# Large GpSimd operations of an S5 mixer moved to VectorE, its small ones issued later, one gate strip moved behind the GLU

## The chip, the cores and the metric

One core of one Trainium2 chip. The metric is the device time of one execution of the program, in microseconds (us), lower is better. The core's engines are TensorE (PE in the rows, its weight loads PEld), VectorE (DVE), ScalarE (ACT), GpSimd (POOL) and SyncE (SP, which issues nearly all DMAs). Each runs its own instructions in a fixed order; semaphores tie them together.

## What is computed

A decoder layer on 1024 tokens of width 1024, all in fp32:

```
u_a, u_b, gate_a, gate_b = split(rms_norm(x) @ w_in + b_in)   # 4, 8, 8 and 8 strips of 128 columns
y  = s5(u_a)                  # complex diagonal recurrence, 32 groups, 64 states each
z  = gelu(y);  ya = z * sigmoid(z @ w_glu + b_glu)
xc = conv4(u_b);  r, i = sigmoid(xc @ w_r), sigmoid(xc @ w_i)   # per head
a  = exp(-8 r softplus(-lambda));  h_t = a h_(t-1) + sqrt(1 - a^2) i xc
m  = sigmoid(gate_a) * (ya @ w_a_out) + sigmoid(gate_b) * (h @ w_b_out)
x1 = x + m @ w_o;  x2 = x1 + swiglu(rms_norm(x1));  then a gated per-layer embedding and a last norm
```

The S5 parameters are made on the chip: `dt`, `mag = exp(lam_re*dt)`, sine and cosine of `lam_im*dt`, the powers of the complex step (`ar9`, `ai9`), and `fr, fi`, which need a division by `den = lam_re^2 + lam_im^2`.

## The kernel before, in words

**Layout.** Everything is held feature-major, as tiles of 128 partitions x 1024 tokens. A product of fp32 matrices is made of three products of split values (high and low part: `whi`, `wlo`, `xgh`, `xgl`). A strip of 128 output columns takes 8 blocks of 128 input rows, in two chunks of four; a chunk is loaded by SP, its high part made by ACT (L187), its low part by DVE (L188).

**Units.** TensorE's work is a list of units that `emit` (L320) writes out in order. u0 to u7 are the per-layer embedding's product; u8 to u11 the four `u_a` strips; then come `GATES_FIRST` = 10 gate strips (u12 to u21), four GLU units, one gate strip, eight `w_a_out` units, and eight `u_b` strips, each but the first followed by the small `r, i` product of the strip before it (`ri_mm` L586) and some by a gate strip (`UB_GATES`, after the strips 1, 3 and 5); then a gate strip, the last `r, i` product, and the last gate strip. After that come `w_b_out`, `w_o`, the feed-forward and the embedding's gate. Every unit's result is taken out of PSUM (its evacuation) only after the next unit's first chunk has been written out; PSUM has 4 buffers for units.

**Chains.** After each chunk `emit` calls `tick` (L244), and `tick` moves each running generator on by one `yield`. So the work beside the strips is written out in steps, one for each chunk: the norm's chain (`rstd_chain` L367), the S5 mixer (`s5_all` L1119 with `s5_params`, `s5_setup`, `s5_data`) and the recurrence (`lru` L605).

**Order on an engine.** A planner orders the instructions of each engine; what is written out first goes first among what is ready. All tiles of 128 x 1024 come from one pool of 43 buffers, and a buffer is given out in the order in which the tiles are written out. So an operation that needs a new tile can't go ahead of the tiles written out before it, such as the evacuation of the strip before. `high_priority` moves an instruction up, `issue_after(i)` holds one back until `i` was issued. The first 10 units have ACT and DVE in written order.

**The norm.** x is squared and summed on ACT and DVE (L410, L412), TensorE sums over partitions (L377), DVE scales it (L384), POOL takes the power -0.5 (L385), DVE spreads the result to a diagonal (L386), TensorE broadcasts it (L392), ACT copies it out as `rb`. TensorE has L392 between u8 and u9.

**S5.** `s5_params` works on 128 x 16 tiles, on POOL: two exponentials (L1062 to L1081), x and th (L1157), sine and cosine (L1163 to L1189), quadrants (L1192 on), powers (L1217 on), `den` and its reciprocal on DVE (L1241 to L1244), `fr`, `fi`, and the split angle `gh`, `gl` (L1259 to L1270): seven steps. Then a loop waits until the norm's result is known (`while "x" not in self.rstd`). Then: `bb` (L1279), `bd`, and `s5_setup` for each of two halves in five steps: the products `qr`; `qi` (DVE) and `wr, wi` (POOL, L1327 to L1332); transposes (L1343); small products (L1358); `ks`, with the DMAs of `km`. Then `s5_data` in seven steps for each half: loads and tables (L1384 to L1392 DVE, `m8` L1394, L1395 POOL), sine and cosine (ACT), `psv` (PE), four products (DVE L1437 to L1440) and sums (POOL L1442, L1443), two scans (L1445, L1446), four products (L1447 to L1450) and sums (POOL L1451, L1452), `psy` (PE L1465, L1470), and the store of Y. The second half runs one step behind the first. The units of the GLU are preceded by `pre_glu` (L666), which writes out all steps that S5 still has, then loads y, makes z = gelu(y) and splits it.

**Recurrence.** `lru` takes two strips at a time: a, a tanh (ACT), a squared (POOL L616), L619 (DVE), L621 and L626 (POOL), and the scan L630 (DVE).

Of the kernel before, what the change touches and what calls it, by code (L numbers as in the profile page):

```python
# [17 lines left out]
P = 128  # L18
# [15 lines left out]
GATES_FIRST = 10  # L34
UB_GATES = (1, 3, 5)
# [59 lines left out]
class Build:  # L95
# [271 lines left out]
    def rstd_chain(self, acc, put, n=L, lag=0, lag2=0):  # L367
# [67 lines left out]
    def plan(self):  # L435
# [169 lines left out]
        def lru(m0):  # L605
# [19 lines left out]
            for m in ms:  # L625
                nc.gpsimd.tensor_tensor(out=ri[m, 1], in0=ri[m, 1], in1=th.pop(m), op=ALU.mult)  # L626
# [25 lines left out]
        def load_z():  # L652
            for m in range(4):
# [4 lines left out]
                self.zs[m] = self.split(z, "z")  # L658
                yield
# [71 lines left out]
        def ev_b(m):  # L731
            def ev(ps):
# [6 lines left out]
                nc.gpsimd.tensor_tensor(out=g, in0=g, in1=gl.pop(("p", m)), op=ALU.add)  # L739
# [379 lines left out]
    def s5_all(self):  # L1119
        self.zs = {}  # L1120
# [23 lines left out]
    def s5_params(self):  # L1144
# [45 lines left out]

        n, b, hh = T("n"), T("b"), T("hh")
        e.tensor_scalar(out=n, in0=k, scalar1=0.25, scalar2=-0.375, op0=ALU.mult, op1=ALU.add)  # L1192
        e.tensor_scalar(out=n, in0=n, scalar1=MAGIC, scalar2=None, op0=ALU.add)
        e.tensor_scalar(out=n, in0=n, scalar1=-MAGIC, scalar2=-4.0, op0=ALU.add, op1=ALU.mult)
        e.tensor_tensor(out=n, in0=k, in1=n, op=ALU.add)
        e.tensor_scalar(out=hh, in0=n, scalar1=2.0, scalar2=None, op0=ALU.is_ge)
        e.tensor_scalar(out=b, in0=hh, scalar1=-2.0, scalar2=None, op0=ALU.mult)
        e.tensor_tensor(out=b, in0=n, in1=b, op=ALU.add)
        nb, ss, cs, sn, cn, w2 = T("nb"), T("ss"), T("cs"), T("sn"), T("cn"), T("w2")
        e.tensor_scalar(out=nb, in0=b, scalar1=-1.0, scalar2=1.0, op0=ALU.mult, op1=ALU.add)  # L1200
        e.tensor_scalar(out=ss, in0=hh, scalar1=-2.0, scalar2=1.0, op0=ALU.mult, op1=ALU.add)
        e.tensor_scalar(out=cs, in0=b, scalar1=-2.0, scalar2=1.0, op0=ALU.mult, op1=ALU.add)
        e.tensor_tensor(out=cs, in0=cs, in1=ss, op=ALU.mult)
        e.tensor_tensor(out=sn, in0=s, in1=nb, op=ALU.mult)
        e.tensor_tensor(out=w2, in0=c, in1=b, op=ALU.mult)
        e.tensor_tensor(out=sn, in0=sn, in1=w2, op=ALU.add)
        e.tensor_tensor(out=sn, in0=sn, in1=ss, op=ALU.mult)
        e.tensor_tensor(out=cn, in0=c, in1=nb, op=ALU.mult)
        e.tensor_tensor(out=w2, in0=s, in1=b, op=ALU.mult)
        e.tensor_tensor(out=cn, in0=cn, in1=w2, op=ALU.add)  # L1210
        e.tensor_tensor(out=cn, in0=cn, in1=cs, op=ALU.mult)
        yield

        ar9 = self.ar9 = self.small([P, 16, 9], name="ar9")
        ai9 = self.ai9 = self.small([P, 16, 9], name="ai9")
        pw = self.small([P, 16, 4], name="pw")
        e.memset(ar9[:, :, 0:1], 1.0)  # L1217
        e.memset(ai9[:, :, 0:1], 0.0)
        ar, ai = ar9[:, :, 1], ai9[:, :, 1]
        e.tensor_tensor(out=ar, in0=mag, in1=cn, op=ALU.mult)  # L1220
        e.tensor_tensor(out=ai, in0=mag, in1=sn, op=ALU.mult)
        for m in (1, 2, 4):

            lo, hi = slice(1, m + 1), slice(m + 1, 2 * m + 1)
            br = ar9[:, :, m:m + 1].to_broadcast([P, 16, m])
            bi = ai9[:, :, m:m + 1].to_broadcast([P, 16, m])
            e.tensor_tensor(out=ar9[:, :, hi], in0=ar9[:, :, lo], in1=br, op=ALU.mult)
            e.tensor_tensor(out=pw[:, :, :m], in0=ai9[:, :, lo], in1=bi, op=ALU.mult)
            e.tensor_tensor(out=ar9[:, :, hi], in0=ar9[:, :, hi], in1=pw[:, :, :m], op=ALU.subtract)
            e.tensor_tensor(out=ai9[:, :, hi], in0=ar9[:, :, lo], in1=bi, op=ALU.mult)  # L1230
            e.tensor_tensor(out=pw[:, :, :m], in0=ai9[:, :, lo], in1=br, op=ALU.mult)
            e.tensor_tensor(out=ai9[:, :, hi], in0=ai9[:, :, hi], in1=pw[:, :, :m], op=ALU.add)
        self.mag8 = T("mag8")
        e.tensor_tensor(out=self.mag8, in0=mag, in1=mag, op=ALU.mult)
        e.tensor_tensor(out=self.mag8, in0=self.mag8, in1=self.mag8, op=ALU.mult)
        e.tensor_tensor(out=self.mag8, in0=self.mag8, in1=self.mag8, op=ALU.mult)
        yield

        nr, den, fr, fi = T("nr"), T("den"), T("fr"), T("fi")
        e.tensor_scalar(out=nr, in0=ar, scalar1=-1.0, scalar2=None, op0=ALU.add)  # L1240
        e.tensor_tensor(out=den, in0=lr, in1=lr, op=ALU.mult)  # L1241
        e.tensor_tensor(out=w, in0=li, in1=li, op=ALU.mult)
        e.tensor_tensor(out=den, in0=den, in1=w, op=ALU.add)
        nc.vector.reciprocal(out=den, in_=den)  # L1244
        e.tensor_tensor(out=fr, in0=nr, in1=lr, op=ALU.mult)
        e.tensor_tensor(out=w, in0=ai, in1=li, op=ALU.mult)
        e.tensor_tensor(out=fr, in0=fr, in1=w, op=ALU.add)
        e.tensor_tensor(out=fr, in0=fr, in1=den, op=ALU.mult)
        e.tensor_tensor(out=fi, in0=ai, in1=lr, op=ALU.mult)
        e.tensor_tensor(out=w, in0=nr, in1=li, op=ALU.mult)  # L1250
        e.tensor_tensor(out=fi, in0=fi, in1=w, op=ALU.subtract)
        e.tensor_tensor(out=fi, in0=fi, in1=den, op=ALU.mult)

        gh, gl, rh, rl = (T(q) for q in ("gh", "gl", "rh", "rl"))
        self.gh, self.gl = gh, gl
        C = 4.0 / math.pi
        ch = round(C * 2048) / 2048
        cl = C - ch
        e.tensor_scalar(out=gh, in0=r, scalar1=C, scalar2=MAGIC / 8192, op0=ALU.mult, op1=ALU.add)  # L1259
        e.tensor_scalar(out=gh, in0=gh, scalar1=-MAGIC / 8192, scalar2=None, op0=ALU.add)  # L1260
        e.tensor_scalar(out=rh, in0=r, scalar1=MAGIC / 4096, scalar2=None, op0=ALU.add)
        e.tensor_scalar(out=rh, in0=rh, scalar1=-MAGIC / 4096, scalar2=None, op0=ALU.add)
        e.tensor_tensor(out=rl, in0=r, in1=rh, op=ALU.subtract)
        e.tensor_tensor(out=rl, in0=rl, in1=re, op=ALU.add)
        e.tensor_scalar(out=gl, in0=rh, scalar1=ch, scalar2=None, op0=ALU.mult)
        e.tensor_tensor(out=gl, in0=gl, in1=gh, op=ALU.subtract)
        e.tensor_scalar(out=w, in0=rl, scalar1=C, scalar2=None, op0=ALU.mult)
        e.tensor_tensor(out=gl, in0=gl, in1=w, op=ALU.add)
# [27 lines left out]
    def s5_setup(self, hf):  # L1296
# [77 lines left out]
    def s5_tables(self, hf):  # L1374
# [19 lines left out]
        nc.gpsimd.tensor_scalar(out=m8, in0=it, scalar1=0.0, scalar2=None, op0=ALU.is_gt)  # L1394
        nc.gpsimd.tensor_tensor(out=m8, in0=m8, in1=G(self.mag8), op=ALU.mult)  # L1395
# [153 lines left out]
```

## Time and profile before

| | |
|---|---|
| median of 3 runs | 1478.7 us (1478.49 to 1478.82) |
| the profiled execution | 1479.04 us, its span 1477.0 us |
| busy | PE 96%, DVE 58%, ACT 38%, POOL 22% of the span |
| mean granted TensorE clock | 0.979 of full speed |

The profiled execution's own time is 2.04 us longer than its span: what lies around the span. In the rows, a line of a timeline is start, duration, engine, line of the kernel, operation, output and inputs with their sizes, and in brackets the engine's idle time before it with what ended it. A granted clock of 1.00 is TensorE's upper level, 2.4 GHz; the lower level is 1.2 GHz.

### The profile page before, as it was taken

Reading aid. Unit: us, or ns where it says so; the run is one execution under the profiler, and the core shown is the slowest. Engines: PE = TensorE matmul, PEld = TensorE weight load, DVE = VectorE, ACT = ScalarE, POOL = GpSimd, SP = SyncE. Lnnn points to the kernel's source line nnn. Section 1 sums busy time; section 2 is a strip of 40 time slices with the busy share of each in tenths; the row PEclk is TensorE's granted clock in tenths of the full one; section 3 lists DMA queues with packets and bytes.
Section 4 is the critical chain, followed back from the end, with each engine's and each line's share of the span. In section 5 each row is a group of like instructions: output and inputs, shape, how many; then the busy total and the mean of one; then the engine's idle time right before and its main releaser. Section 6 shows DMA issues by size and latency. Waiting matters only on the chain.

```text
span 1477.0 us, 16858 instructions
## 1 busy us (share of the span) xinstructions
PE 1420.7 (96%) x6586; PEld 1174.8 (80%) x6586; DVE 862.3 (58%) x938; ACT 554.1 (38%) x711; POOL 320.6 (22%) x314
## 2 busy tenths in 40 slices
PE   8689999999999799999999999999999999999995
PEld 6478878788888688887788888888888888888885
DVE  6284693555588983366555566665556234266486
ACT  7132233612555731244433333333335342133333
POOL 7980641410243532100000000000000021012243
PEclk9799999999999899999999999999999999999997
DMA  8123424372212154342122222222217442232222
GB/s 320 46 92 100 130 86 118 103 270 72 64 58 65 50 204 138 124 168 94 57 86 86 87 86 86 86 86 86 85 59 259 143 156 69 72 107 93 72 93 114
DMA packets 70319, 161.39 MB, mean 109 GB/s; under 512 B 11521, under 2 KB 23201, under 8 KB 70241
## 3 DMA queue, kind: packets, MB, share of 16 engines
q1 hardware_dynamic: 70240, 160.33, 32.4%
q8 instruction: 51, 0.84, 0.2%
q14 instruction: 28, 0.22, 0.0%
HBM read 118.23 MB, written 40.89 MB: 108 GB/s over the span
## 4 chain that ended last, share of the span: by engine, by line
PE 77%; DVE 9%; issue 5%; POOL 5%; ACT 2%; SPq 1%; DMA 1%; DVEq 0%; POOLq 0%; ACTq 0%
PE mm L220 44%; PE mm L312 28%; PE sm L220 1%; DVE wlo L188 1%; PE sm L1470 1%; PE sm L1465 1%; DVE xc L579 1%; DVE x L1028 1%; SPq L1369 1%; PE sm L392 0%; POOL el L1027 0%; SPq L1480 0%; ACT sq L410 0%; DVE el L1018 0%; DMA s5p<-s5p 0%
## 5 line engine op out<-in xcount | busy, mean ns | idle before, releaser
L187 ACT ACTIVATE whi<-raw 128x512 fp32r<-128x512 f32 (+1 forms) x158 | 96.8, 617 | 336.6 <-PE mm L220 283.3
L188 DVE TENSOR_TENSOR wlo<-raw,whi 128x512 fp32r<-128x512 f32 (+1 forms) x158 | 144.4, 917 | 133.2 <-ACT whi L187 133.0
L312 PE MATMUL mm<-twh,whi 128*128 128x512 f32 x528 | 206.4, 391 | 1.3 <-ACT pc L290 1.0
L312 PE MATMUL mm<-twl,whi 128*128 128x512 f32 x528 | 206.0, 390 | 0.8 <-DVE twl L232 0.8
L312 PE MATMUL mm<-twh,wlo 128*128 128x512 f32 x528 | 202.5, 390 | 0.0
L412 POOL TENSOR_TENSOR acc<-acc,sq 128x1024 f32<-128x1024 f32 (+1 forms) x18 | 42.7, 2371 | 612.3 <-ACT sq L410 612.3
L220 PE MATMUL mm<-xgh,whi 128*128 128x512 f32 x448 | 142.2, 398 | 0.0
L220 PE MATMUL mm<-xgh,wlo 128*128 128x512 f32 x448 | 139.6, 394 | 0.8 <-DVE wlo L188 0.8
L220 PE MATMUL mm<-xgl,whi 128*128 128x512 f32 x448 | 140.2, 394 | 0.0
L312 PEld LDWEIGHTS mm<-twh,whi 128*128 128x128 f32 x528 | 99.4, 188 | 23.0 <-ACT pc L290 1.4
L312 PEld LDWEIGHTS mm<-twl,whi 128*128 128x128 f32 x528 | 99.4, 188 | 21.9 <-DVE twl L232 1.1
L312 PEld LDWEIGHTS mm<-twh,wlo 128*128 128x128 f32 x528 | 99.4, 188 | 20.7
L220 PE MATMUL mm<-vh,wlo 128*128 128x512 f32 x352 | 108.9, 390 | 0.0
L174 ACT ACTIVATE whi<-wr 128x512 fp32r<-128x512 f32 x110 | 69.5, 631 | 105.1 <-PE mm L312 101.6
L220 PE MATMUL mm<-vl,whi 128*128 128x512 f32 x352 | 108.4, 389 | 0.0
L220 PE MATMUL mm<-vh,whi 128*128 128x512 f32 x352 | 108.3, 389 | 0.0
L220 PEld LDWEIGHTS mm<-xgh,whi 128*128 128x128 f32 x448 | 85.4, 191 | 19.2 <-issue 1.4
L220 PEld LDWEIGHTS mm<-xgh,wlo 128*128 128x128 f32 x448 | 85.1, 190 | 19.0 <-DVE wlo L188 1.2
L220 PEld LDWEIGHTS mm<-xgl,whi 128*128 128x128 f32 x448 | 85.5, 191 | 18.2 <-issue 0.2
L175 DVE TENSOR_TENSOR wlo<-wr,whi 128x512 fp32r<-128x512 f32 x110 | 74.6, 686 | 26.6 <-ACT whi L174 26.5
L220 PEld LDWEIGHTS mm<-vh,wlo 128*128 128x128 f32 x352 | 66.1, 188 | 14.0 <-issue 0.2
L220 PEld LDWEIGHTS mm<-vh,whi 128*128 128x128 f32 x352 | 66.1, 188 | 13.9 <-issue 0.2
(390 smaller groups left out, 2580.1 us busy)
## 6 DMA issues: line engine op xcount, KB each, us to landing
raw<-w_in SPq DMA_DIRECT2D x56, 256.0 KB, 2.9
wr<-w_gate SPq DMA_DIRECT2D x22, 512.0 KB, 5.1
wr<-w_up SPq DMA_DIRECT2D x22, 512.0 KB, 3.6
vd<-fv SPq DMA_DIRECT2D x22, 512.0 KB, 3.0
vr<-vd SPq DMA_DIRECT2D x22, 512.0 KB, 5.1
raw<-w_down SPq DMA_DIRECT2D x32, 256.0 KB, 2.7
el<-ed SPq DMA_DIRECT2D x16, 512.0 KB, 4.2
x<-xT SPq DMA_DIRECT2D x8, 512.0 KB, 7.1
```

What stands on the lines that cost most here:

```text
L174: nc.scalar.activation(out=hi, in_=src, func=AF.Copy)
L175: nc.vector.tensor_tensor(out=lo, in0=src, in1=hi.bitcast(F32), op=ALU.subtract)
L187: nc.scalar.activation(out=hi[:, :w], in_=raw[:, :w], func=AF.Copy)
L188: nc.vector.tensor_tensor(out=lo[:, :w], in0=raw[:, :w], in1=hi[:, :w].bitcast(F32), op=ALU.subtract)
L220: nc.tensor.matmul(ps[:, t - t0:e - t0], w, v[:, t:e], start=(first and q == 0), stop=(last and q == 2),)
L312: nc.tensor.matmul(bank[b], w[:, k * P:(k + 1) * P], v, start=start and k == 0 and p == 0, stop=k == 3 and p == 2, skip_group_check=True)
L412: eng.tensor_tensor(out=a, in0=a, in1=s, op=ALU.add)
L579: nc.vector.scalar_tensor_tensor(out=xc[:, s:], in0=u[:, :L - s], scalar=self.v("conv_w", 8 * (3 - s) + m), in1=xc[:, s:], op0=ALU.mult, o ...
L1028: nc.vector.tensor_tensor(out=x, in0=x, in1=e, op=ALU.add)
L1369: nc.sync.dma_start(km[i][16 * j:16 * j + 16, :, (7 - j) * 16:P], ks[16 * i:16 * i + 16, :, 0:(j + 1) * 16])
L1465: nc.tensor.matmul(ps[:, o:o + P], km[hh][:, pr, :], us[q][:, 2 * i + hh, :], start=True, stop=False)
L1470: nc.tensor.matmul(ps[:, o + 1:o + P], G(w[hs, pr]), x[hs, pr * P:pr * P + 127], start=False, stop=last)
```

## The change

- Moved from POOL to DVE: the six operations of `wr, wi` in each half of `s5_setup`; `m8` (two operations become one); the sums L1442, L1443 and L1451, L1452; in the recurrence L621 and L626; the GLU's product L677; the sum L739 behind `w_b_out`. The square L616 goes from POOL to ACT.
- z is kept in fp32 (`self.zf`), so that the sum `zh + zl` (L676) goes.
- `den` is made at S5's first step, and its reciprocal on DVE is written out at the third step in place of the seventh.
- The small operations from L1192 to L1270 (65 on POOL, two of them memsets: quadrants, powers, `fr, fi`, `gh, gl`) are written out after the loop that waits for the norm, in four steps, and `issue_after(self.rs)` holds them behind the norm's power on POOL.
- `s5_setup` has one `yield` more in each half, between `qi` and `wr, wi`.
- `GATES_FIRST` goes from 10 to 9, `UB_GATES` from (1, 3, 5) to (1, 2, 4, 5).
- The mark that holds back the recurrence's small parameters is the last memset of `km` in place of the last operation of `wi`.

```diff
-GATES_FIRST = 10
-UB_GATES = (1, 3, 5)
+GATES_FIRST = 9
+UB_GATES = (1, 2, 4, 5)
...
-            nc.gpsimd.tensor_tensor(out=rs[:, :m], in0=ms[:, :m], in1=self.mhalf[:, :m], op=ALU.pow)
+            self.rs = nc.gpsimd.tensor_tensor(out=rs[:, :m], in0=ms[:, :m], in1=self.mhalf[:, :m], op=ALU.pow).ins
...
-                nc.gpsimd.tensor_tensor(out=a2[m], in0=a[m], in1=a[m], op=ALU.mult)
+                nc.scalar.activation(out=a2[m], in_=a[m], func=AF.Square)
...
-                nc.gpsimd.tensor_tensor(out=ri[m, 1], in0=ri[m, 1], in1=xct.pop(m), op=ALU.mult)
+                nc.vector.tensor_tensor(out=ri[m, 1], in0=ri[m, 1], in1=xct.pop(m), op=ALU.mult)
...
-                nc.gpsimd.tensor_tensor(out=ri[m, 1], in0=ri[m, 1], in1=th.pop(m), op=ALU.mult)
+                nc.vector.tensor_tensor(out=ri[m, 1], in0=ri[m, 1], in1=th.pop(m), op=ALU.mult)
...
                 self.zs[m] = self.split(z, "z")
+                self.zf[m] = z
...
-                zh, zl = self.zs[m]
-                z = self.slot(name="z")
-                nc.gpsimd.tensor_tensor(out=z, in0=zh.bitcast(F32), in1=zl.bitcast(F32), op=ALU.add)
-                nc.gpsimd.tensor_tensor(out=s, in0=s, in1=z, op=ALU.mult)
+                nc.vector.tensor_tensor(out=s, in0=s, in1=self.zf.pop(m), op=ALU.mult)
...
-                nc.gpsimd.tensor_tensor(out=g, in0=g, in1=gl.pop(("p", m)), op=ALU.add)
+                nc.vector.tensor_tensor(out=g, in0=g, in1=gl.pop(("p", m)), op=ALU.add)
...
         nc.sync.dma_start(self.bc, h["s5bc"])
+        den, dw = T("den"), T("dw")
+        e.tensor_tensor(out=den, in0=lr, in1=lr, op=ALU.mult)
+        e.tensor_tensor(out=dw, in0=li, in1=li, op=ALU.mult)
+        e.tensor_tensor(out=den, in0=den, in1=dw, op=ALU.add)
         yield
         dt = self.exp_accurate(e, ldt, sh)
         yield
+        nc.vector.reciprocal(out=den, in_=den)
...
         while "x" not in self.rstd:
             yield
+        with self.tc.issue_after(self.rs):
+
+            n, b, hh = T("n"), T("b"), T("hh")
...
+        yield
+        with self.tc.issue_after(self.rs):
+
+            ar9 = self.ar9 = self.small([P, 16, 9], name="ar9")
...
+        yield
+        with self.tc.issue_after(self.rs):
+
+            nr, fr, fi = T("nr"), T("fr"), T("fi")
...
+        yield
+        with self.tc.issue_after(self.rs):
+
+            gh, gl, rh, rl = (T(q) for q in ("gh", "gl", "rh", "rl"))
...
+        yield
...
         e.tensor_tensor(out=qi, in0=qi, in1=t, op=ALU.add)
-
-        e = g
+        yield
+
         wr, wi, t = mk("wr"), mk("wi"), mk("wt")
...
-        nc.gpsimd.tensor_scalar(out=m8, in0=it, scalar1=0.0, scalar2=None, op0=ALU.is_gt)
-        nc.gpsimd.tensor_tensor(out=m8, in0=m8, in1=G(self.mag8), op=ALU.mult)
+        nc.vector.scalar_tensor_tensor(out=m8, in0=it, scalar=0.0, in1=G(self.mag8), op0=ALU.is_gt, op1=ALU.mult)
...
-        nc.gpsimd.tensor_tensor(out=qr, in0=qr, in1=t1, op=ALU.add)
-        nc.gpsimd.tensor_tensor(out=qi, in0=qi, in1=t2, op=ALU.subtract)
+        nc.vector.tensor_tensor(out=qr, in0=qr, in1=t1, op=ALU.add)
+        nc.vector.tensor_tensor(out=qi, in0=qi, in1=t2, op=ALU.subtract)
...
-        nc.gpsimd.tensor_tensor(out=qr, in0=qr, in1=si, op=ALU.subtract)
-        nc.gpsimd.tensor_tensor(out=qi, in0=qi, in1=co, op=ALU.add)
+        nc.vector.tensor_tensor(out=qr, in0=qr, in1=si, op=ALU.subtract)
+        nc.vector.tensor_tensor(out=qi, in0=qi, in1=co, op=ALU.add)
```

## Rows read from the trace of the kernel before

**Rows 1.** Waits of TensorE in 0 to 600 us: us in total, times, longest.

```profile
PE sm L377 <- DVE acc L412: 8.6, 1, 8.6
...
PE sm L1343 <- DVE qi L1321: 3.7, 1, 3.7
```

**Rows 2.** Timeline of VectorE around the norm.

```profile
42.91 0.25 DVE L1244 RECIPROCAL den<-den 128x16 f32<-128x16 f32 x1 [8.22 <-POOL den L1243]
...
61.07 1.64 DVE L386 TENSOR_TENSOR dg<-ident,rs 128x1024 f32<-128x1024 f32 x1 [10.59 <-POOL rs L385]
```

**Rows 3.** Timeline of TensorE around the norm.

```profile
46.73 3.54 PE L377 MATMUL sm<-ones,acc 128*128 128x1 f32 x16 [8.59 <-DVE acc L412]
...
62.85 3.59 PE L392 MATMUL sm<-dg,ones 128*128 128x512 f32 x4 [5.19 <-DVE dg L386]
65.62 1.27 PE L220 MATMUL mm<-xgh,whi 128*128 128x512 f32 x2
```

**Rows 4.** Timeline of GpSimd around the norm.

```profile
39.80 0.25 POOL L1260 TENSOR_SCALAR gh<-gh 128x16 f32<-128x16 f32 x1
...
59.37 1.67 POOL L385 TENSOR_TENSOR rs<-ms,mhalf 128x8 f32<-128x8 f32 x1
```

**Rows 5.** Timeline of VectorE, gate strips and S5's data.

```profile
122.76 1.22 DVE L523 TENSOR_TENSOR ga<-mm,rb 128x1024 f32<-128x1024 f32 x1 [4.43 <-PE mm L220]
...
133.64 1.23 DVE L523 TENSOR_TENSOR ga<-mm,rb 128x1024 f32<-128x1024 f32 x1 [4.49 <-PE mm L220]
...
150.72 1.23 DVE L523 TENSOR_TENSOR ga<-mm,rb 128x1024 f32<-128x1024 f32 x1 [4.06 <-PE mm L220]
...
162.47 1.22 DVE L1384 TENSOR_TENSOR ph<-iota,gh 128x1024 f32<-128x1024 f32 x1
...
172.21 1.21 DVE L1389 TENSOR_TENSOR ph<-ph,pw 128x1024 f32<-128x1024 f32 x1
...
190.10 3.38 DVE L1389 TENSOR_TENSOR ph<-ph,pw 128x1024 f32<-128x1024 f32 x1
...
227.99 1.22 DVE L1449 TENSOR_TENSOR ph<-q,ph 128x1024 f32<-128x1024 f32 x1
```

**Rows 6.** Timeline of TensorE, S5's last products and the GLU's first.

```profile
240.74 1.05 PE L1465 MATMUL sm<-U,km 128*128 128x128 f32 x8
...
249.10 0.71 PE L1470 MATMUL sm<-q,wi 64*128 64x127 f32 x8
...
265.73 1.65 PE L220 MATMUL mm<-zh,whi 128*128 128x512 f32 x6 [0.93 <-ACT zh L231]
```

**Rows 7.** Timeline of TensorE, the last r, i product.

```profile
494.75 1.22 PE L220 MATMUL sm<-xch,whi 128*128 128x512 f32 x2 [6.78 <-ACT xch L231]
497.18 1.22 PE L220 MATMUL sm<-xch,whi 128*128 128x512 f32 x2 [1.21 <-ACT ri L599]
...
503.20 0.62 PE L220 MATMUL mm<-xgh,wlo 128*128 128x512 f32 x2
```

**Rows 8.** Chain of waits, the same sum at a later norm.

```profile
692.35 1.92 PE sm L377 x16
```

**Rows 9.** Stretches: us, busy and instructions of PE, PEld, DVE, ACT, POOL, granted clock, DMA.

```profile
8.70:34.80 26.10, 25.31 (x105) 20.40 (x105) 22.24 (x21) 23.01 (x26) 23.25 (x41) 1.00 0.91 352
34.80:59.30 24.50, 14.27 (x51) 11.48 (x49) 5.09 (x7) 0.00 (x0) 22.69 (x98) 0.72 0.16 59
162.40:229.30 66.90, 64.19 (x412) 53.63 (x411) 64.77 (x58) 19.94 (x21) 31.17 (x12) 0.95 0.31 96
175.00:200.00 25.00, 25.00 (x155) 20.85 (x155) 24.90 (x26) 10.23 (x11) 5.32 (x3) 1.00 0.26 82
```

**Rows 10.** Timeline of VectorE before the last r, i product.

```profile
485.12 3.42 DVE L619 SCALAR_TENSOR_TENSOR ri<-a,ri 128x1024 f32<-128x1024 f32 x1
488.46 1.27 DVE L579 SCALAR_TENSOR_TENSOR xc<-u,vec,xc 128x1022 f32<-128x1022 f32 x1
...
490.26 3.35 DVE L579 SCALAR_TENSOR_TENSOR xc<-u,vec,xc 128x1021 f32<-128x1021 f32 x1
```

More of the change, by code (lines that the diff above doesn't have):

```diff
@@ L1119, in s5_all @@
     def s5_all(self):
-        self.zs = {}
+        self.zs, self.zf = {}, {}
         self.s5gen = self.chains[-1]
@@ L1189, in s5_params @@
         yield
[L1191 to L1268, printed above, removed]
@@ L1269, in s5_params @@
-        e.tensor_scalar(out=w, in0=rh, scalar1=cl, scalar2=None, op0=ALU.mult)
-        e.tensor_tensor(out=gl, in0=gl, in1=w, op=ALU.add)
-        yield
         while "x" not in self.rstd:
             yield
+        with self.tc.issue_after(self.rs):
+            n, b, hh = T("n"), T("b"), T("hh")
+            e.tensor_scalar(out=n, in0=k, scalar1=0.25, scalar2=-0.375, op0=ALU.mult, op1=ALU.add)
+            e.tensor_scalar(out=n, in0=n, scalar1=MAGIC, scalar2=None, op0=ALU.add)
+            e.tensor_scalar(out=n, in0=n, scalar1=-MAGIC, scalar2=-4.0, op0=ALU.add, op1=ALU.mult)
+            e.tensor_tensor(out=n, in0=k, in1=n, op=ALU.add)
+            e.tensor_scalar(out=hh, in0=n, scalar1=2.0, scalar2=None, op0=ALU.is_ge)
+            e.tensor_scalar(out=b, in0=hh, scalar1=-2.0, scalar2=None, op0=ALU.mult)
+            e.tensor_tensor(out=b, in0=n, in1=b, op=ALU.add)
+            nb, ss, cs, sn, cn, w2 = T("nb"), T("ss"), T("cs"), T("sn"), T("cn"), T("w2")
+            e.tensor_scalar(out=nb, in0=b, scalar1=-1.0, scalar2=1.0, op0=ALU.mult, op1=ALU.add)
+            e.tensor_scalar(out=ss, in0=hh, scalar1=-2.0, scalar2=1.0, op0=ALU.mult, op1=ALU.add)
+            e.tensor_scalar(out=cs, in0=b, scalar1=-2.0, scalar2=1.0, op0=ALU.mult, op1=ALU.add)
+            e.tensor_tensor(out=cs, in0=cs, in1=ss, op=ALU.mult)
+            e.tensor_tensor(out=sn, in0=s, in1=nb, op=ALU.mult)
+            e.tensor_tensor(out=w2, in0=c, in1=b, op=ALU.mult)
+            e.tensor_tensor(out=sn, in0=sn, in1=w2, op=ALU.add)
+            e.tensor_tensor(out=sn, in0=sn, in1=ss, op=ALU.mult)
+            e.tensor_tensor(out=cn, in0=c, in1=nb, op=ALU.mult)
+            e.tensor_tensor(out=w2, in0=s, in1=b, op=ALU.mult)
+            e.tensor_tensor(out=cn, in0=cn, in1=w2, op=ALU.add)
+            e.tensor_tensor(out=cn, in0=cn, in1=cs, op=ALU.mult)
@@ new lines, in s5_params @@
+        yield
+        with self.tc.issue_after(self.rs):
+            ar9 = self.ar9 = self.small([P, 16, 9], name="ar9")
+            ai9 = self.ai9 = self.small([P, 16, 9], name="ai9")
+            pw = self.small([P, 16, 4], name="pw")
+            e.memset(ar9[:, :, 0:1], 1.0)
+            e.memset(ai9[:, :, 0:1], 0.0)
+            ar, ai = ar9[:, :, 1], ai9[:, :, 1]
+            e.tensor_tensor(out=ar, in0=mag, in1=cn, op=ALU.mult)
+            e.tensor_tensor(out=ai, in0=mag, in1=sn, op=ALU.mult)
+            for m in (1, 2, 4):
+                lo, hi = slice(1, m + 1), slice(m + 1, 2 * m + 1)
+                br = ar9[:, :, m:m + 1].to_broadcast([P, 16, m])
+                bi = ai9[:, :, m:m + 1].to_broadcast([P, 16, m])
+                e.tensor_tensor(out=ar9[:, :, hi], in0=ar9[:, :, lo], in1=br, op=ALU.mult)
+                e.tensor_tensor(out=pw[:, :, :m], in0=ai9[:, :, lo], in1=bi, op=ALU.mult)
+                e.tensor_tensor(out=ar9[:, :, hi], in0=ar9[:, :, hi], in1=pw[:, :, :m], op=ALU.subtract)
+                e.tensor_tensor(out=ai9[:, :, hi], in0=ar9[:, :, lo], in1=bi, op=ALU.mult)
+                e.tensor_tensor(out=pw[:, :, :m], in0=ai9[:, :, lo], in1=br, op=ALU.mult)
+                e.tensor_tensor(out=ai9[:, :, hi], in0=ai9[:, :, hi], in1=pw[:, :, :m], op=ALU.add)
+            self.mag8 = T("mag8")
+            e.tensor_tensor(out=self.mag8, in0=mag, in1=mag, op=ALU.mult)
+            e.tensor_tensor(out=self.mag8, in0=self.mag8, in1=self.mag8, op=ALU.mult)
+            e.tensor_tensor(out=self.mag8, in0=self.mag8, in1=self.mag8, op=ALU.mult)
@@ new lines, in s5_params @@
+        yield
+        with self.tc.issue_after(self.rs):
+            nr, fr, fi = T("nr"), T("fr"), T("fi")
+            e.tensor_scalar(out=nr, in0=ar, scalar1=-1.0, scalar2=None, op0=ALU.add)
+            e.tensor_tensor(out=fr, in0=nr, in1=lr, op=ALU.mult)
+            e.tensor_tensor(out=w, in0=ai, in1=li, op=ALU.mult)
+            e.tensor_tensor(out=fr, in0=fr, in1=w, op=ALU.add)
+            e.tensor_tensor(out=fr, in0=fr, in1=den, op=ALU.mult)
+            e.tensor_tensor(out=fi, in0=ai, in1=lr, op=ALU.mult)
+            e.tensor_tensor(out=w, in0=nr, in1=li, op=ALU.mult)
+            e.tensor_tensor(out=fi, in0=fi, in1=w, op=ALU.subtract)
+            e.tensor_tensor(out=fi, in0=fi, in1=den, op=ALU.mult)
@@ new lines, in s5_params @@
+        yield
+        with self.tc.issue_after(self.rs):
+            gh, gl, rh, rl = (T(q) for q in ("gh", "gl", "rh", "rl"))
+            self.gh, self.gl = gh, gl
+            C = 4.0 / math.pi
+            ch = round(C * 2048) / 2048
+            cl = C - ch
+            e.tensor_scalar(out=gh, in0=r, scalar1=C, scalar2=MAGIC / 8192, op0=ALU.mult, op1=ALU.add)
+            e.tensor_scalar(out=gh, in0=gh, scalar1=-MAGIC / 8192, scalar2=None, op0=ALU.add)
+            e.tensor_scalar(out=rh, in0=r, scalar1=MAGIC / 4096, scalar2=None, op0=ALU.add)
+            e.tensor_scalar(out=rh, in0=rh, scalar1=-MAGIC / 4096, scalar2=None, op0=ALU.add)
+            e.tensor_tensor(out=rl, in0=r, in1=rh, op=ALU.subtract)
+            e.tensor_tensor(out=rl, in0=rl, in1=re, op=ALU.add)
+            e.tensor_scalar(out=gl, in0=rh, scalar1=ch, scalar2=None, op0=ALU.mult)
+            e.tensor_tensor(out=gl, in0=gl, in1=gh, op=ALU.subtract)
+            e.tensor_scalar(out=w, in0=rl, scalar1=C, scalar2=None, op0=ALU.mult)
+            e.tensor_tensor(out=gl, in0=gl, in1=w, op=ALU.add)
+            e.tensor_scalar(out=w, in0=rh, scalar1=cl, scalar2=None, op0=ALU.mult)
+            e.tensor_tensor(out=gl, in0=gl, in1=w, op=ALU.add)
@@ L1331, in s5_setup @@
         e.tensor_tensor(out=t, in0=ai, in1=cr, op=ALU.mult)
-        self.mark = [e.tensor_tensor(out=wi, in0=wi, in1=t, op=ALU.subtract).ins, None]
+        e.tensor_tensor(out=wi, in0=wi, in1=t, op=ALU.subtract)
         st["w", hf] = (wr, wi)
@@ L1335, in s5_setup @@
         for k in km:
-            g.memset(k, 0.0)
+            self.mark = [g.memset(k, 0.0).ins, None]
         yield
```

## The prediction

> **What bounds the kernel now.** The table's busy shares come first: TensorE is busy for nearly the whole span, so the time is its work plus its few waits. The list of its waits says where those are [rows 1]: the first 600 us hold the two largest, and both hang on engines that the change touches. The timelines of the head say why. VectorE stands 8.22 us before the reciprocal of `den`, which POOL delivers late [rows 2], and behind it in written order stands the last sum of squares. So TensorE starts the sum over partitions at 46.73 after 8.59 us of waiting, and L392 at 62.85 after 5.19 more [rows 3], because the power runs on POOL only at 59.37, when the last small S5 operation is done [rows 4]. Next I read how S5 follows the strips [rows 5], then the join: the GLU's second block starts at 265.73 and had waited only 0.93 us for z [rows 6]. S5 is thus just in time now; whatever delays it, TensorE will wait for. The last r, i product waits 6.78 and 1.21 us [rows 7].
>
> **The head.** The reciprocal is no longer waited for: L377 goes from 46.73 to 46.73 - 8.22 = 38.5. At the upper clock it takes 1.92 us [rows 8] in place of 3.54, so the scaled sum is there at some 40.6. POOL must still finish both exponentials, the sine and cosine. In 34.8 to 59.3 it ran 98 operations [rows 9]; 60 of those are moved behind the power (65 less two memsets and the three that ran sooner), two belong to `den`, now earlier: 36 remain. Beside a working VectorE one took 26.1/41 = 0.64 us, beside an idle one 24.5/98 = 0.25 us [rows 9]. Three moved operations fewer and two of `den` more before 34.8 put POOL at the same point near 33.4; until 38.5 it does 8, then 28 at 0.25: the power at 45.5. From the power to L392 is 62.85 - 59.37 = 3.48, from there to the next strip 2.77 [rows 3, 4]. So u9 starts at 51.8 in place of 65.62: **-13.8**. Bounds: with POOL free at 40.6 it is 46.9 (-18.7); with all 36 at 0.64 it is 62.7 (-2.9). I take 45.5, since VectorE will idle, as it does in the second stretch. What is late next is the power itself.
>
> **S5's steps.** After the norm's result one step is written out per chunk. Before: two steps, then five for each half, so that the loads and tables are step 13, which is u15's first chunk, after the evacuation of u14. After: four steps for the small operations, two, then six for each half: the tables are step 19, u18's first chunk, after the evacuation of u17. Step and time agree in the trace: `gh` was there at 40.05 [rows 4], yet the product that needs only it and a constant ran at 162.47, one strip after u14's evacuation at 150.72, although VectorE had waits of over 4 us before every strip's evacuation [rows 5]. Steps bind, not operands.
>
> A strip takes 133.64 - 122.76 = 10.88, one with a half's transposes and small products 150.72 - 133.64 = 17.08, so these cost 6.20 [rows 5]. The model gives u14's end before as 65.6 + 6 x 10.88 + 2 x 6.20 + 3.7 (the wait for `qi` [rows 1]) + 2.8 (slow restart, below) = 149.8, which is 0.9 short. After: the new step between `qi` and the transposes takes that wait away, so u17 ends at 51.8 + 9 x 10.88 + 12.4 + 0.9 = 163.0. With the same 162.47 - 150.72 = 11.75 behind it, the tables start at 174.8, which is 12.3 later than now. Bound: 163.0 if the 11.75 vanish.
>
> **S5's data on VectorE.** Now from 162.47 to 229.2: 66.7 us, VectorE busy 64.77 of 66.9 [rows 5, 9]. The same operation took 1.21 alone and 3.38 beside a GpSimd operation [rows 5]; eight operations of the stretch were longer than their twins, by 11.4 in all: -11.4. Ten operations of 1.22 are added (two `m8`, four sums, four differences): +12.2. Fewer strips lie beside it: about five operations of 1.1 less, -5.3. That gives 62.2, so it ends at 237.0. S5's last products follow: 249.81 - 240.74 = 9.1 [rows 6], plus 2.8 since TensorE will have stood before them; then from their end to the GLU's second block 265.73 - 249.81 = 15.9, for Y's store and load, gelu and split. Sum: **264.8 in place of 265.73**, -0.9. A slow restart costs 2.8: after the last r, i product's waits seven pairs of matmuls took 6.02 us, up to 503.20 [rows 7], where a pair takes 0.45 in a strip of 24 (10.88). That is the lower level of the clock (1.2 GHz); the head's stretch with its two waits was granted 0.72 on the mean [rows 9].
>
> TensorE itself is done with its nine strips earlier: 264.8 (the GLU's start less its wait) - 13.8 - 6.5 (wait and restart at `qi`) - 10.9 (the strip moved) = 233.6. So a **new wait of some 31 us** stands before the GLU, around S5's last products. PSUM's four unit buffers go to the four GLU units in written order, so the strip moved behind them can't fill it: it costs its **10.9**, and the restart at the GLU **2.8**.
>
> **The recurrence.** Beside POOL two operations before the last r, i product took 3.42 and 3.35, where a twin takes 1.27 [rows 10]; 4.2 come back. Against it, four operations of 1.22 move to VectorE there, partly into its idle time, and two squares to ACT ahead of the strip's bias. I take **-4**: the wait shrinks to some 3. Bounds: all of 6.78 + 1.21 + 2.8 = 10.8 gone; or four times 1.22 on the path, +0.7. The order of the gates among the `u_b` strips leaves this place as it is.
>
> **For nothing:** the GLU's product and the sum behind `w_b_out` (1.22 each on VectorE, beside 10.88 us of TensorE work a unit; without that cover 5 and 10 us); z in fp32 (four buffers held longer); `m8` as one operation is counted above; the mark moves to a memset that POOL, now idle, runs at once. No DMA is added on SP; U's loads and `km`'s stay with their steps.
>
> The **sum**: -0.9 + 2.8 + 10.9 - 4 = +8.8. The profiled execution took 1479.04 (0.34 above the median of 1478.7): 1487.8 against it, 1487.5 as a median.
>
> **The rivals.** (A) Faster: S5 keeps pace, because the planner sets its operations ahead of the strips written before them. Place: the tables. Price: the 31 us wait and its restart vanish, 1487.5 - 34 = 1453.5; half of it 1470. It decides from a GLU start under 256. For it: VectorE's waits before every evacuation [rows 5] leave room. Against it: that room was there before and the tables weren't in it. (B) The 11.75 us between evacuation and tables vanish: 1475.8. For it: they depend on what the planner put in between. (C) Slower by more: VectorE is the bound and GpSimd wasn't what stretched its operations; the 11.4 stay, 1498.9. VectorE was busy 24.90 of 25 us in the densest stretch [rows 9], though there TensorE waited for nothing. The Trainium skill ("Perfetto Trace Analysis", section "Optimizing Scalar/DVE Operations") says that work may be taken off a saturated VectorE, even to GpSimd, which speaks against this change, but adds that the two share a read port, so that a move between them might not help. By its first half this rival is right, by its second the forecast; the 3.38 against 1.21 agrees with the second. (D) The change doesn't do what it says: the planner leaves the power behind the small operations, or POOL is slower with the rest. Then only the reciprocal's 8.2 of the 13.8 is gained: 1493.1.
>
> **How the numbers follow.** Forecast 0.45, by its bounds 1478 to 1498; A 0.28; B 0.10; C 0.07; D 0.10. A measurement of this kernel tells 0.2% (3.0 us) from no change. Faster: A 0.28, most of B 0.07, 0.05 of the forecast: 0.40. Same: 0.03 of B, 0.08 of the forecast: 0.11. Slower: 0.32 of the forecast, C and D: 0.49. The range 1460 to 1498 leaves out A's far half (about 0.14) and a little above.
>
> **What would show it.** The reciprocal without a wait, L377 near 38.5, the power before the quadrant operations; the tables behind the evacuation of the sixth gate strip, near 175; VectorE's 128 x 1024 products all near 1.22; TensorE idle for some 30 us before the GLU, whose blocks follow near 265; the wait for `xch` at about 3 us. Tables before 163, or a GLU start under 256, would prove the forecast wrong; a GLU start over 275 would speak for C or D.

## The result, and the profile after

The changed kernel takes **1489.45 us** (median of 4 runs, 1487.14 to 1490.51) against 1478.76 for the kernel before on the same chip (1478.49 to 1478.96): 1.007 of it, 95% interval 1.0053 to 1.0088. It is slower by 10.7 us, where 1487.5 was forecast. The profiled execution took 1488.67; its span is 1486.7, which is 9.7 longer than before.

TensorE's waits in 0 to 600 us, in the columns of [rows 1]:

```profile
PE sm L1473 <- DVE q L1454: 12.4, 2, 12.0
PE mm L220 <- ACT zh L231: 10.3, 2, 6.8
PE sm L220 <- ACT xch L231: 6.3, 2, 3.5
...
PE sm L392 <- DVE dg L386: 3.9, 1, 3.9
PE sm L220 <- ACT ri L599: 2.9, 2, 1.7
...
PE sm L377 <- DVE acc L412: 0.2, 1, 0.2
```

The 8.6 us wait of the head is down to 0.2, and the 3.7 at the transposes is gone. In their place stand 12.4 us before S5's last products and 10.3 for z; the waits of the r, i products have become two of each kind. Before, the wait for z was 0.93 [rows 6], and that before S5's last products was this:

```profile
PE sm L1470 <- POOL q L1451: 2.7, 1, 2.7
```

TensorE's timeline answers to [rows 3, 6, 7]:

```profile
38.45 1.92 PE L377 MATMUL sm<-ones,acc 128*128 128x1 f32 x16 [0.17 <-DVE acc L412]
...
48.88 3.65 PE L392 MATMUL sm<-dg,ones 128*128 128x512 f32 x4 [3.85 <-DVE dg L386]
51.56 1.43 PE L220 MATMUL mm<-xgh,whi 128*128 128x512 f32 x2
...
204.78 0.39 PE L220 MATMUL mm<-xgh,wlo 128*128 128x512 f32 x1
217.15 0.80 PE L1473 MATMUL sm<-q,wr 64*128 64x127 f32 x4 [11.98 <-DVE q L1454]
217.73 0.64 PE L1473 MATMUL sm<-q,wi 64*128 64x127 f32 x4
...
235.78 0.39 PE L1473 MATMUL sm<-q,wi 64*128 64x127 f32 x4
...
251.91 2.93 PE L220 MATMUL mm<-zh,whi 128*128 128x512 f32 x6 [6.82 <-ACT zh L231]
...
262.27 1.67 PE L220 MATMUL mm<-zh,whi 128*128 128x512 f32 x6 [3.52 <-ACT zh L231]
...
421.83 1.22 PE L220 MATMUL sm<-xch,whi 128*128 128x512 f32 x2 [2.86 <-ACT xch L231]
424.26 1.22 PE L220 MATMUL sm<-xch,whi 128*128 128x512 f32 x2 [1.21 <-ACT ri L599]
...
505.40 0.73 PE L220 MATMUL sm<-xch,whi 128*128 128x512 f32 x2 [3.46 <-ACT xch L231]
507.83 1.22 PE L220 MATMUL sm<-xch,whi 128*128 128x512 f32 x2 [1.70 <-ACT ri L599]
```

The strips begin 14.1 us earlier (51.56 for 65.62) and are through at 205.2; then TensorE has S5's last products alone, and the GLU's second block starts at 262.27. That is only 3.5 us earlier than before, although one strip of 10.9 fewer stands ahead of it besides. VectorE and then GpSimd show why, against [rows 2, 4, 5]:

```profile
21.76 0.24 DVE L1158 RECIPROCAL den<-den 128x16 f32<-128x16 f32 x1
...
162.91 1.23 DVE L523 TENSOR_TENSOR ga<-mm,rb 128x1024 f32<-128x1024 f32 x1 [4.06 <-PE mm L220]
...
174.66 1.22 DVE L1388 TENSOR_TENSOR ph<-iota,gh 128x1024 f32<-128x1024 f32 x1
...
182.51 1.22 DVE L1393 TENSOR_TENSOR ph<-ph,pw 128x1024 f32<-128x1024 f32 x1
...
198.88 1.22 DVE L1393 TENSOR_TENSOR ph<-ph,pw 128x1024 f32<-128x1024 f32 x1
...
234.19 1.22 DVE L1454 TENSOR_TENSOR q<-q,ph 128x1024 f32<-128x1024 f32 x1
```

```profile
45.81 1.67 POOL L385 TENSOR_TENSOR rs<-ms,mhalf 128x8 f32<-128x8 f32 x1
47.45 0.20 POOL L1198 TENSOR_SCALAR n<-k 128x16 f32<-128x16 f32 x1
```

The power stands ahead of the quadrants, at 45.81. The product that needs `gh` alone still runs one strip after an evacuation, now u17's, 12.2 us later than before. Both halves' L1393 take 1.22, where one took 3.38 beside GpSimd. VectorE's and TensorE's stretches after (columns as in [rows 9]):

```profile
174.60:235.50 60.90, 48.48 (x323) 39.61 (x321) 60.16 (x63) 15.43 (x16) 0.23 (x1) 0.80 0.25 75
...
205.00:262.00 57.00, 34.52 (x207) 27.72 (x206) 31.63 (x30) 15.95 (x14) 0.00 (x0) 0.70 0.31 79
```

S5's data takes VectorE 60.9 us in place of 66.9, with five instructions more. In the second stretch TensorE was busy 34.52 of 57 us, and the granted clock was 0.70 on the mean: four products of one shape took 0.64 at 217.73, after the long wait, and 0.39 at 235.78.

### The profile page after: what moved, and what is told of

The parts are those of the page before. It is cut to its first block, busy times and chain, and to the rows that moved or that the text cites. A ratio compares the mean times of both kernels' runs of the same rounds, so it can differ in the third digit from the quotient of the medians.

```text
span 1486.7 us, 16789 instructions
## 1 busy us (share of the span) xinstructions
PE 1423.7 (96%) x6586; PEld 1175.3 (79%) x6586; DVE 847.3 (57%) x988; ACT 564.3 (38%) x720; POOL 151.3 (10%) x250
## 4 chain that ended last, share of the span: by engine, by line
PE 78%; DVE 7%; issue 5%; ACT 4%; POOL 4%; DMA 1%; SPq 1%; DVEq 0%; ACTq 0%; POOLq 0%
PE mm L220 47%; PE mm L312 28%; PE sm L220 1%; POOL x L963 1%; SPq L1483 1%; PE sm L392 0%; DVE x L1026 0%; DVE xc L579 0%; ACT ri L599 0%; DVE el L1016 0%; PE sm L1473 0%; ACT sq L410 0%; PE sm L377 0%; DMA s5p<-s5p 0%; DVE yb L630 0%
## 5 line engine op out<-in xcount | busy, mean ns | idle before, releaser
L312 PE MATMUL mm<-twh,whi 128*128 128x512 f32 x528 | 206.5, 391 | 1.3 <-ACT pc L290 1.0
L312 PE MATMUL mm<-twl,whi 128*128 128x512 f32 x528 | 206.0, 390 | 0.8 <-DVE twl L232 0.8
L312 PE MATMUL mm<-twh,wlo 128*128 128x512 f32 x528 | 202.7, 390 | 0.0
L188 DVE TENSOR_TENSOR wlo<-raw,whi 128x512 fp32r<-128x512 f32 (+1 forms) x158 | 109.6, 696 | 128.8 <-ACT whi L187 128.8
L312 PEld LDWEIGHTS mm<-twh,whi 128*128 128x128 f32 x528 | 99.5, 188 | 23.1 <-ACT pc L290 1.4
L312 PEld LDWEIGHTS mm<-twl,whi 128*128 128x128 f32 x528 | 99.5, 189 | 22.0 <-DVE twl L232 1.1
L312 PEld LDWEIGHTS mm<-twh,wlo 128*128 128x128 f32 x528 | 99.4, 188 | 20.8
```

The costliest lines, as they stand in the source:

```text
L188: nc.vector.tensor_tensor(out=lo[:, :w], in0=raw[:, :w], in1=hi[:, :w].bitcast(F32), op=ALU.subtract)
L312: nc.tensor.matmul(bank[b], w[:, k * P:(k + 1) * P], v, start=start and k == 0 and p == 0, stop=k == 3 and p == 2, skip_group_check=True)
```

## The experiments

Each was timed beside the kernel before on the same chip. Its median was 1478.04 (1476.0 to 1479.82, 18 runs) beside the first four, 1478.07 beside the next four and 1478.22 beside the last three; single runs of one kernel lay up to 8 us apart (e2_gates), so that 2 us between two medians say little.

**Do the added steps make S5 late?** e1_steps takes four `yield` lines out again. The last of the four small blocks keeps its own, and the line in `s5_setup` counts for both halves, so that five of the six added steps go, as the 14 in place of 19 below has it:

```diff
-        yield
         with self.tc.issue_after(self.rs):
             ar9 = self.ar9 = self.small([P, 16, 9], name="ar9")
...
         e.tensor_tensor(out=qi, in0=qi, in1=t, op=ALU.add)
-        yield
```

> The changed kernel with the six added steps taken out again: the four blocks of small S5 operations are written out in one step behind the norm's power, and no step stands between qi and wr, wi. All moves to VectorE, the gates and the early power stay. Theory (steps bind): the loads and tables are step 14 in place of 19, behind the evacuation of u14; they start near 51.7 + 6 x 10.88 + 12.4 + 0.9 + 11.75 = 142 in place of 174.66, S5 is done before the strips, the 12.0 us and 10.3 us of waits before the GLU vanish, its second block starts near 233 in place of 262.3: 1489 - 29 = 1460 (1455 to 1466). Rival (VectorE is the bound, or the operations moved to it make S5 late): tables earlier or not, the time stays at 1484 to 1491.

Measured: 1474.26 (1473.36 to 1475.3), 0.9973 of before (0.9963 to 0.9983); 15.2 us less than the changed kernel. The tables start at 141.85 for the 142 expected, and the rival falls. The number agrees better than its parts: u14's evacuation came 4.6 us sooner than I took it, and the tables start 16.2 us behind it in place of 11.75, since step 14 is u15's second chunk:

```profile
125.67 1.22 DVE L523 TENSOR_TENSOR ga<-mm,rb 128x1024 f32<-128x1024 f32 x1 [5.17 <-PE mm L220]
...
141.85 1.22 DVE L1384 TENSOR_TENSOR ph<-iota,gh 128x1024 f32<-128x1024 f32 x1
```

But the gain is half of what was expected. TensorE's and SP's timelines say where it stopped:

```profile
212.69 0.49 PE L1469 MATMUL sm<-q,wr 64*128 64x127 f32 x4 [0.52 <-DVE q L1450]
...
242.46 2.93 PE L220 MATMUL mm<-zh,whi 128*128 128x512 f32 x6 [17.54 <-ACT zh L231]
```

```profile
218.62 15.48 SPq L1479 DMA_DIRECT2D yd<-Y  x32
234.20 0.38 SPq L655 DMA_DIRECT2D y<-yd  x1
```

The tables start 32.8 us sooner than in the changed kernel, S5's last sum ends only 22.8 sooner, at 212.6: with strips beside it, S5's data takes 70.8 us in place of 60.75. And z is ready 30 us later still: SP issues the 32 stores of Y one after the other in 15.48 us, and the first load of y stands behind all of them. I had left both out of the expectation, since I had taken S5 to be ahead of the strips.

**The gates.** e2_gates sets `GATES_FIRST = 10` and `UB_GATES = (1, 3, 5)` in the changed kernel.

> The changed kernel with the gate strips as before (ten before the GLU, one after the u_b strips 1, 3 and 5). Theory (S5 is late, TensorE waits for it): the tables stay near 174.7 and the GLU's second block near 262, the tenth strip fills part of the wait before the GLU, so that everything behind gains 10.9; the new wait at the r, i product of strip 5 (2.9 + 1.2 and a slow restart, some 7) goes if the order of the gates made it. Together 1471 to 1479. Rival (the strip was worth more behind the GLU, or the wait grows with it): 1486 to 1492.

Measured: 1474.96 (1470.79 to 1478.88), ratio 0.9971 (0.995 to 0.9992). The tables stay at 174.45, the second block of the GLU at 264.39, and a whole strip lies under the wait. There is no wait at the product of strip 3 (the expectation calls it strip 5; the order of the units makes it 3, counted from 0); the last product waits 4.11 and 1.69. As expected.

e7_gates makes the same edit the other way round, in the kernel before: `GATES_FIRST = 9`, `UB_GATES = (1, 2, 4, 5)`.

> The kernel before with the changed gates alone: nine strips before the GLU, the others after the u_b strips 1, 2, 4 and 5. Theory: S5 ends within 5 us of where it ends now, so the strip behind the GLU costs 6 to 11; two u_b strips without a gate between them make a wait at the r, i product of strip 3 of 3 to 7 us with its restart; the last r, i product waits as before: 1487 to 1497. Rival (S5 keeps pace, a strip is worth the same anywhere, and the gates relieve the u_b strips): 1474 to 1480.

Measured: 1492.46 (1491.46 to 1492.95), ratio 1.0098 (1.0083 to 1.0113): **the gates alone cost 14.4 us**. The GLU waits for z, and the r, i products show two waits, as in the changed kernel:

```profile
260.73 2.93 PE L220 MATMUL mm<-zh,whi 128*128 128x512 f32 x6 [5.66 <-ACT zh L231]
...
421.37 0.73 PE L220 MATMUL sm<-xch,whi 128*128 128x512 f32 x2 [2.17 <-ACT xch L231]
...
505.19 0.73 PE L220 MATMUL sm<-xch,whi 128*128 128x512 f32 x2 [3.78 <-ACT xch L231]
```

Here POOL still works beside VectorE, and yet the last wait is 3.78 in place of 6.78: the order of the gates had part in it, which I had excluded, for this run too.

**The head.** e3_recip is the kernel before with `den` at the first step and the reciprocal at the third.

> The kernel before with den computed at S5's first step and its reciprocal at the third, nothing else. If the wait for the reciprocal alone held the head, the sum over partitions and all behind it move by 8.2 us, S5's steps with it: 1470.5. If POOL's 98 small operations hold the power, it stays near 59 and the time within 2 us of 1478.7, with the 8.6 us wait at L377 turned into a longer one at L392.

Measured: 1478.69 (1476.59 to 1481.21), ratio 1.0005 (0.9996 to 1.0015): nothing. GpSimd's power and TensorE's L392:

```profile
59.24 1.67 POOL L385 TENSOR_TENSOR rs<-ms,mhalf 128x8 f32<-128x8 f32 x1
```

```profile
62.73 3.75 PE L392 MATMUL sm<-dg,ones 128*128 128x512 f32 x4 [17.48 <-DVE dg L386]
```

The wait for the reciprocal alone was not the head's bound: with it gone, GpSimd's queue held the power as late as before. One wait of 17.48 us took the place of two.

e4_head adds the early power, with the small operations behind it in one step; GpSimd keeps its large operations.

> The kernel before with the changed s5_params alone: early den and reciprocal, the small operations behind the power, but written out in one step. POOL keeps all its large operations, the gates stay. Theory: the power runs near 45.8, u9 starts 13.9 us earlier, and S5 is one step (half a strip, 5.4 us) later against the strips, with no slack at the GLU: 1478.7 - 13.9 + 5.4 = 1470 (1465 to 1474). Rival (S5 loses to POOL what the head gains, since the small operations now run behind the power): 1477 to 1482.

Measured: 1467.38 (1465.86 to 1468.92), ratio 0.9926 (0.9912 to 0.9941). As the theory has it: the gain of the head comes through, less a wait for z of 5.31.

**The moves to VectorE.** e5_s5dve adds S5's moves to e4_head, e6_lrudve the recurrence's.

> The kernel of e4_head with S5's large operations on VectorE as well (wr and wi, m8, the sums), without the step added in s5_setup. In e4_head S5's last sum ends on POOL at 220.95, 7.3 us after VectorE's last operation. Theory (VectorE's work there stays the same, since the ten added operations cost what the contention gives back): the last sum ends 5 to 8 us earlier, the waits for zh (5.3 and 1.1 us, with a slow restart) shrink: 1459 to 1465. Rival (the added operations make VectorE the bound): the last sum ends 5 to 11 us later, 1471 to 1478.

> The kernel of e4_head with the recurrence's operations moved (the square to ACT, the two products to VectorE). The waits at the last r, i product were 6.8 + 1.2 with POOL; in e2_gates, with the same order of the gates and the moves, 4.1 + 1.7. Theory: some 2 us less, 1464 to 1467. Rival (the four operations of 1.22 on VectorE and the squares lengthen the way to xc): 1468 to 1472.

Measured: 1458.79 (1456.82 to 1460.28, ratio 0.987, 0.9855 to 0.9885) and 1464.68 (1463.18 to 1465.76, ratio 0.991, 0.9895 to 0.9925). So S5's moves gain 8.6, the recurrence's 2.7. The second is as expected (waits of 4.1 and 1.7). The first has the expected size and another place: S5's last sum ends 10.5 us sooner (210.49 for 220.95), but the wait for z stays, 5.23 for 5.31, since TensorE arrives sooner by as much. The same stretch in e4_head, then in e5_s5dve:

```profile
140.00:215.00 75.00, 69.71 (x436) 58.15 (x436) 68.86 (x61) 19.77 (x22) 35.66 (x34) 0.95 0.33 100
```

```profile
140.00:215.00 75.00, 75.00 (x476) 63.12 (x475) 68.31 (x72) 26.32 (x28) 7.58 (x17) 1.00 0.33 103
```

VectorE is busy for the same time with 72 instructions in place of 61, and TensorE, which lost 5.3 us beside GpSimd, loses none. In e4_head it had waited inside the stretch until VectorE had done its products that read PSUM, such as here:

```profile
198.63 0.71 PE L1468 MATMUL sm<-U,km 128*128 128x128 f32 x4 [2.03 <-DVE q L1443]
```

e5_s5dve takes two things away at once: what GpSimd did to VectorE's operations beside it, and GpSimd's own sums, which took 2.35 to 3.32 us each in e4_head where VectorE takes 1.22. No run parts the two.

**All of it, and the steps again.** e9_all is the changed kernel with the gates as before and, as in e1_steps, without five of the six added steps; e11_four puts the three steps between the small blocks back.

> The changed kernel with the gates as before and with the six added steps taken out (the small operations in one step): early power and all moves to VectorE. It differs from e5_s5dve by the recurrence's moves and those of the GLU and of the sum behind w_b_out. Theory: the recurrence's moves are worth what they were in e6_lrudve (2.7), the others nothing: 1458.8 - 2.7 = 1456 (1453 to 1459). Rival (the moves in GLU and w_b_out cost, or the gains overlap): 1459 to 1464.

> The kernel of e9_all with the small operations in four steps again, nothing else: three steps more before the tables. With one step the tables stood at 142 (e1_steps), with six more and an order alike at 174.5 (e2_gates, 1475.0). Theory (each step puts S5 off by half a strip): tables near 142 + 3 x 5.4 = 158, and the time between e9_all and e2_gates: e9_all + 6 to 13. Rival (only the step inside s5_setup hurts, since it parts VectorE's work): within 2 us of e9_all.

Measured: 1458.66 (1457.83 to 1459.8, ratio 0.9865, 0.9848 to 0.9881) and 1464.57 (1459.87 to 1465.9, ratio 0.9896, 0.9876 to 0.9916). e9_all lies with e5_s5dve (1458.79): the gain of the recurrence doesn't reach the end. In the profiled executions it is there up to the next norm, whose sum (L377) starts at 666.91 in e9_all and at 670.66 in e5_s5dve. It is lost right behind: the 20 us from that sum on were granted 0.74 in e9_all and 0.91 in e5_s5dve, the norm's broadcast (L392) took 3.64 us and 1.96, and at the last product of L312 0.5 of the 3.75 is left (1095.2 and 1095.7). Why the clock stayed low for longer there is not shown. The moves in the GLU and behind `w_b_out` cost nothing that can be seen. In e11_four three steps more put the tables from 139.96 to 162.03, which is later than the 158 expected, and cost 5.9, where 6 to 13 were expected. VectorE in e9_all, then in e11_four:

```profile
123.78 1.22 DVE L523 TENSOR_TENSOR ga<-mm,rb 128x1024 f32<-128x1024 f32 x1 [5.17 <-PE mm L220]
...
139.96 1.22 DVE L1384 TENSOR_TENSOR ph<-iota,gh 128x1024 f32<-128x1024 f32 x1
```

```profile
150.28 1.23 DVE L523 TENSOR_TENSOR ga<-mm,rb 128x1024 f32<-128x1024 f32 x1 [4.06 <-PE mm L220]
...
162.03 1.22 DVE L1387 TENSOR_TENSOR ph<-iota,gh 128x1024 f32<-128x1024 f32 x1
```

The 22 us are two whole strips: step 14 is u15's second chunk, behind the evacuation of u14, step 17 is u17's first, behind that of u16; what counts is the evacuation ahead, not the half strip. With e2_gates (step 19, behind u17, one strip more) that makes three points: tables at 140, 162 and 174 go with 1458.7, 1464.6 and 1475.0. The first 22 us cost 5.9, so they are mostly free; the last 12 cost 10.4, almost their full length.

**Two tries for more.** e8_stores gives every second store of Y to ACT's queue, in e4_head; e10_gates11 is e9_all with `GATES_FIRST = 11`, `UB_GATES = (2, 5)`.

> The kernel of e4_head with every second of the 32 stores of Y issued on ACT's queue in place of SP's. In every run so far 16 stores of a half take 7.4 to 8.5 us to issue on SP, and the loads of y stand behind them. Theory (the way from S5's last product to z is bound by these issues): the second half's z comes 3 to 4 us earlier, the wait for zh of 5.3 shrinks to under 2: 1461 to 1465. Rival (the transfers themselves or the gelu bind): within 1.5 us of e4_head, 1466 to 1469.

> The kernel of e9_all with eleven gate strips before the GLU and the others after the u_b strips 2 and 5. Theory: the 5.2 us wait for zh and its restart are filled by the strip (-5 to -8), but with fewer gates among the u_b strips there is one wait more for xc (+4 to +8): within 4 us of e9_all. Rival (the u_b strips have slack enough): e9_all - 8 to - 5.

Measured: e8_stores 1468.18 (1465.94 to 1470.57), the rival's outcome. The issues of a half do take half as long, but the loads of y come no sooner (245.73; 246.12 in e4_head), and ACT's own work now stands behind its eight issues:

```profile
236.47 4.08 SPq L1483 DMA_DIRECT2D yd<-Y  x8
245.27 0.35 SPq L161 DMA_DIRECT2D raw<-w_a_out  x1
245.73 1.42 SPq L655 DMA_DIRECT2D y<-yd  x3
```

```profile
236.47 4.26 ACTq L1483 DMA_DIRECT2D yd<-Y  x8
240.76 1.28 ACT L657 ACT_TABLE_LOAD   x1 [3.40 <-DMA yd<-Y]
```

What held the loads back until 245.73 is the line ahead of them: in SP's order a load of weights stands before them, and by the trace it waited 4.3 us for a buffer that VectorE's L188 was still to read. So e8_stores shows neither that the issues bind the tail nor that they don't.

e10_gates11: **1456.5** (1456.41 to 1458.4), ratio 0.985 (0.9836 to 0.9865), the fastest that was run: 22 us under before, 33 under the changed kernel. Against e9_all it is 2.2 less, which the spread of the runs leaves open. The wait for z falls from 6.1 to 2.2, a second one appears at an r, i product, as expected.

## Why the prediction was right, and where it was not

| step | forecast | measured |
|---|---|---|
| sum over partitions starts | 38.5 | 38.45 |
| power on GpSimd | 45.5 | 45.81 |
| first strip behind the norm | 51.8 | 51.56 |
| evacuation of u17 | 163.0 | 162.91 |
| first operation of the tables | 174.8 | 174.66 |
| VectorE's last sum ends | 237.0 | 235.41 |
| GLU's second block | 264.8 + 2.8 | 262.27 |
| waits of the recurrence, to the end | -4 | +2.3 |
| whole time against the profiled execution | +8.8 | +9.6 |

**The head** held to 0.3 us, and for the reason given: what is late next is the power, behind GpSimd's remaining operations. e3_recip shows that the reciprocal alone is worth nothing, e4_head that it is worth the whole head together with the order on GpSimd; the order alone was not run. Rival D (the power stays late) falls, and its price, 8.2 for the reciprocal alone, was wrong.

**S5's steps** are shown by dose: e1_steps, e11_four, e2_gates and the changed kernel differ in steps and gates, and the tables follow the evacuation that the count puts ahead of them. Rival A (S5 keeps pace) falls, and so does B: from u17's evacuation to the tables it is 11.75 us, as before. The prediction had counted in evacuations and was within 0.2 us; the half strip a step that I wrote for e11_four is the coarser rule.

**Contention** gave back what the ten operations cost: 60.75 us from the first operation of the tables to the last sum, 62.2 forecast. Rival C falls: with GpSimd out of the way VectorE did more instructions in the same busy time (e5_s5dve). The forecast's "1.21 alone" was misread: beside that operation too a GpSimd one ran (L1395, from 172.42, for 2.76 us), so an operation beside GpSimd is not stretched each time. The sum goes by the eight stretched ones and doesn't hang on it, and in the changed kernel the same operation takes 1.22 in both halves. Of the rule of the Trainium skill ("Perfetto Trace Analysis", section "Optimizing Scalar/DVE Operations") the second half agrees, that work moved between the two may gain nothing: here the way back, off GpSimd, gained 8.6 us. No run shows the port. What I had not seen is the place of the gain, TensorE's waits for PSUM inside the strips.

**The wait before the GLU** came where it was forecast, and e2_gates shows that a strip fits under it. It was some 31 us by the forecast; from 205.2 to 262.27 TensorE idled 11.98 + 0.45 + 6.82 + 3.52 = 22.8 us, and the stretch was granted 0.70. The terms there were too dear by 5.3 together (267.6 less 262.27). Two restarts of 2.8 were charged and neither was paid: the slow products from 217.15 on ran while VectorE still worked on the second half, and the GLU's slow first block, at 251.91, ended before z was there for the second. VectorE was 1.6 sooner; against that, from its last sum to the second block it took 26.9 in place of 9.1 + 15.9.

**The recurrence** is the step that failed: "The order of the gates among the `u_b` strips leaves this place as it is" is true for none of the two places. The last wait shrank (3.46 + 1.70 for 6.78 + 1.21), but a new one stands at the product of strip 3 (2.86 + 1.21, and a slow restart). From the GLU's second block to the last r, i product (its first line in [rows 7]) it took 243.1 us in place of 229.0, that is the strip of 10.9 and 3.2 more; from there to the end of the span 0.9 came back. That makes +2.3, where -4 had been taken; +0.7 had been my worst bound. e2_gates and e7_gates give the new wait to the order of the gates, since it goes and comes with them and without regard to the moves. The shrinking of the last wait has both causes: to 3.78 by the gates alone (e7_gates), to 4.12 by the moves alone (e6_lrudve), and together hardly further. These two errors, -5.3 and +6.3, nearly cancel: that the sum came within 1 us of the profiled execution is luck.

What the change cost is so divided: its head and its moves are worth 19.6 us (e9_all), its gates and five of its six added steps lose 30.8 (1489.45 less 1458.66).

## What to carry to other kernels

Where work beside a main stream is written out in steps bound to that stream, count the steps before counting microseconds: a step added for order's sake is a transfer of time to whatever waits at the end of the chain, once the slack there is used up. A wait that goes is worth nothing until the next late thing on the path is named, on every engine that feeds it (here GpSimd's queue behind VectorE's reciprocal). And a reordering of filler work among slack places is priced place by place, since it can open one wait while it closes another.

## What the runs showed of the hardware that I had not expected

In e1_steps SP took 15.48 us to issue 32 stores of Y, 0.48 each, with the loads of the same data queued behind. And moving S5's large operations from GpSimd to VectorE (e4_head to e5_s5dve) left VectorE's busy time from 140 to 215 us as it was (68.86 and 68.31), while TensorE's rose from 69.71 to 75.00.
